# Encoder block on one core: where the second feed-forward half's weight operands are made and stored in the first half's loop, and the last norm's gain one tile later

## The chip, the cores and the metric

The kernel runs on one core of a Trainium2 chip. TensorE (PE) multiplies, VectorE (DVE), ScalarE (ACT) and GpSimd (POOL) work element by element, and SyncE (SP) issues most of the transfers between DRAM and SBUF. Each engine takes its instructions in order; between engines there are semaphores. The metric is the device time of one execution in microseconds (us).

## The reference

One transformer layer in float32 on a sequence of 1024 tokens and a width of 1024. Cut to the part that the change touches, the channel sub-layer:

```
h = modulate(layer_norm(x), sh2, sc2)                  # 1024 x 1024
gt, up = jnp.split(h @ w_ffn_in[l], 2, axis=-1)        # 1024 x 2816 each
y = (jax.nn.silu(gt) * up) @ w_ffn_out[l]              # w_ffn_out 2816 x 1024
x = layer_norm(ALPHA * x + g2[:, None, :] * y, ln2_g[l], ln2_b[l])
```

Ahead of it stands the mixer sub-layer (differential attention and multi-scale pooling), which the change leaves alone.

## The kernel before

A float32 product is made of three products of rounded halves: an operand is cast to its high part on ScalarE, VectorE subtracts that from the operand to get the low part (`split`, L96 and L97), and `mm3` multiplies high by high, high by low and low by high (L100 to L102). On top of this both feed-forward products run in Strassen's scheme, with seven products of sums of blocks instead of eight of blocks.

The first half (h times `w_ffn_in`, SiLU, gating) is a loop over 22 pairs f of 128 gate and 128 up columns. Its order on all five engines is written out by hand (`tc.manual_schedule`). Pair f multiplies its own five operands (`prod`, 12 products of 128x128x512 each) and makes the operands of pair n = f + 1 meanwhile: sums of weight blocks (`ws`) on GpSimd and VectorE, then `operand`, a `split` into `oh` and `ol`. From pair 4 (`BR`) on a pair begins with two more chains of 12 products (`first_mm`), so that it has 84 products in place of 60.

At the start of such a pair ScalarE copies the first chain's bank (`first_cp`, L929), VectorE adds the second (`first_add`, L934), and `half_gate` takes a tanh of the sum (L1238). PE can start the chain into the other half of the second bank once that add is done. Then PE's chains and their readers alternate: the copy `u` (L1270) reads bank a, the copy `p5` (L1278) bank c, and PE overwrites a bank when its reader is done. Five operands share four buffers, so the fifth (`operand(f, blocks(f)[3])`) waits until PE has used the first.

The second half multiplies by `w_ffn_out`, and its weight operands are made in this same loop, a piece at a time, by the generator `fw_prep`: for each of 11 rounds k it loads four blocks, makes three differences on GpSimd, and gives seven operands. For each one `op` splits a block into a buffer and returns the store to `wfD` in DRAM. Buffers rotate through four tags:

```python
tag = ("whi", "fwo", "wlo", "fwo")[cnt[0] % 4]
pool, bufs = (fwp, 1) if tag == "fwo" else (wp, 2)
...
split(w[:, 0, :], w[:, 1, :], src)
return lambda: nc.sync.dma_start(wfD[q - 1, k], w.bitcast(F32))
```

`fwo` has one buffer, so every second operand needs the store of the one two steps earlier to have landed. `fw_step` first issues the store that is due (`behind_`), then makes the next operand. Pairs 1 to 3 call it three times, pairs 4 on four times, which makes 77 operands by the end of pair 20. From pair 4 on the first and third operand of a pair are `fwo`. They are called s1 to s4 below.

The second half (L1480 and around it) ends with tiles 4 to 7 of the output, one after the other as PE finishes them: `last_stats` (the residual, L1384 and L1385, and its statistics), `last_norm` (mean, and on GpSimd the root, L437 and L93, and the shift, L1391 and L1392), then `last_half` twice. For tiles 4 to 6 the upper half is normalised on ScalarE (L1396), and GpSimd multiplies by the gain and adds the bias (L1399, L1400); the other halves are done by VectorE (`affine`, L443 and L444). Each half is then sent to the output.

Of the kernel before, what the change touches and what calls it, by code (L numbers as in the profile page):

```python
# [18 lines left out]
P = 128  # L19
# [16 lines left out]
def encoder_block_kernel(  # L36
# [6 lines left out]
    nc = tc.nc  # L43
    x2 = x[0]
    out2 = out[0]
# [159 lines left out]
    with tc.tile_pool(name="pre", bufs=1, reuse_waits="tile") as pre:  # L205
# [15 lines left out]
        for i in range(4):  # L221
            t = pre.tile([P, 2, D], F32, tag="x", bufs=6, name="x%d" % i)
# [218 lines left out]
    def affine(z, st, g, b):  # L441
        m, r = st
        nc.vector.scalar_tensor_tensor(z, z, m[:, 0:1], g, op0=ALU.subtract, op1=ALU.mult)  # L443
        nc.vector.scalar_tensor_tensor(z, z, r, b, op0=ALU.mult, op1=ALU.add)  # L444
# [463 lines left out]
    def prod(ps, w, x, start, stop):  # L908
        for k in range(4):
            mm3(ps, w[0][:, k, :], w[1][:, k, :], x[0][:, k, :], x[1][:, k, :],  # L910
                start and k == 0, stop and k == 3, True)
# [245 lines left out]
    def fw_prep():  # L1157


        wt = {}  # L1160

        def load(k, i, j):
            if k < NK:
                w = fwp.tile([P, HF], F32, tag="fw%d%d" % (i, j), bufs=2 - max(i, j), name="fw%d%d_%d" % (i, j, k))
                nc.sync.dma_start(w, wfo[(i * NK + k) * P:(i * NK + k + 1) * P, j * HF:(j + 1) * HF])
                wt[k, i, j] = w

        cnt = [0]

        def op(q, k, src):  # L1170
            tag = ("whi", "fwo", "wlo", "fwo")[cnt[0] % 4]
            cnt[0] += 1
            pool, bufs = (fwp, 1) if tag == "fwo" else (wp, 2)
            w = pool.tile([P, 2, HF], F32R, tag=tag, bufs=bufs, name="fw%d_%d" % (q, k))
            split(w[:, 0, :], w[:, 1, :], src)
            return lambda: nc.sync.dma_start(wfD[q - 1, k], w.bitcast(F32))

        for ij in ((0, 0), (0, 1), (1, 1), (1, 0)):
            load(0, *ij)
        for k in range(NK):  # L1180
            w11, w12, w21, w22 = [wt.pop((k, *ij)) for ij in ((0, 0), (0, 1), (1, 0), (1, 1))]
            load(k + 1, 0, 0)
            pol(w12, w12, w11, op=ALU.subtract)
            yield op(1, k, w11)
            yield op(3, k, w22)
            pol(w22, w22, w12, op=ALU.subtract)
            yield op(5, k, w12)
            load(k + 1, 0, 1)
            pol(w11, w22, w11, op=ALU.subtract)
            yield op(2, k, w21)  # L1190
            pol(w21, w21, w22, op=ALU.subtract)
            yield op(6, k, w22)
            load(k + 1, 1, 1)
            yield op(7, k, w11)
            yield op(4, k, w21)
            load(k + 1, 1, 0)
# [2 lines left out]

    def fw_step():  # L1200

        if prep is None:
            return
        for store in behind_:
            store()
        behind_[:] = [x for x in [next(prep, None)] if x]


    raws, sums_, wg = {}, {}, {}
# [5 lines left out]
    def load_up(f):  # L1215
        if f < NF:
            raws[f] = raws[f][0], uload(f)

    def blocks(f):
        rawg, rawu = raws[f]  # L1220
        return rawg[:, 0:4, :], rawg[:, 4:8, :], rawu[:, 0:4, :], rawu[:, 4:8, :]

    def operand(f, src):
        o = (fp.tile([P, 4, P], F32R, tag="oh", bufs=4, name="oh%d_%d" % (f, len(ops_.setdefault(f, [])))),
             fp.tile([P, 4, P], F32R, tag="ol", bufs=4, name="ol%d_%d" % (f, len(ops_[f]))))
        split(*o, src)
        ops_[f].append(o)
# [8 lines left out]
    def half_gate(f, half, g):  # L1236
        th = th_tile("th%d_%d" % (f, half))
        nc.scalar.activation(th, g, AF.Tanh, scale=0.5)  # L1238
        halves[f, half] = th, g

    def half_mul(f, half):
        th, g = halves[f, half]
        nc.vector.scalar_tensor_tensor(th, th, 1.0, g, op0=ALU.add, op1=ALU.mult)

    with tc.manual_schedule(engines={nc.vector.engine, nc.gpsimd.engine, nc.tensor.engine, nc.scalar.engine,
                                     nc.sync.engine}):
        load_pair(1)
        load_up(1)
        for f in range(NF):
            n = f + 1  # L1250
            more = n < NF
            if f >= BR:
                first_mm(f, wg.pop(f))
            if more:
                sa, sb = [evp.tile([P, 4, P], F32, tag="st", bufs=2, name="ws%d_%d" % (n, i)) for i in range(2)]
                pol(sa, blocks(n)[2], blocks(n)[3], op=ALU.add)
            if f >= BR:
                first_cp(f)
                fw_step()
                first_add(f, True)  # L1260
            half_gate(f, 0, chain[f][1])
            half_mul(f, 0)
            if f > 0:
                fw_step()
                operand(f, blocks(f)[3])
                a, c11, bc = chain[f]
                c = (ps_s("fc%d" % f) if bc is None else bc)[:, HF:]
                prod(a, ops_[f][0], t2, False, False)
                u2 = ev_tile("u2_%d" % f)
                nc.scalar.copy(u2, a)  # L1270
            load_pair(f + 2)
            if more:
                vec(sb, sa, blocks(n)[0], op=ALU.subtract)
                operand(n, sb)
            if f > 0:
                prod(c, ops_[f][1], t1, True, False)
                p5 = ev_tile("p5_%d" % f)
                nc.scalar.copy(p5, c)  # L1278
            else:
                a, _, c, u2, p5 = chain[f]  # L1280
            if more:
                vec(sb, blocks(n)[1], sb, op=ALU.subtract)
            fw_step()
            prod(a, ops_[f][2], t3, False, False)
            if BR <= n < NF:
                wg[n] = [wp.tile([P, KT, P], F32R, tag=tag, bufs=2, name="wg%d_%s" % (n, tag)) for tag in ("whi", "wlo")]
                nc.scalar.copy(wg[n][0], raws[n][0])
            vec(p5, p5, a, op=ALU.add)
            if more:
                operand(n, sa)  # L1290
                pol(sa, blocks(n)[0], blocks(n)[2], op=ALU.subtract)  # L1291
            if n in wg:
                vec(wg[n][1], raws[n][0], wg[n][0].bitcast(F32), op=ALU.subtract)
            load_up(f + 2)
            prod(c, ops_[f][3], b22, False, True)
            vec(u2, u2, c, op=ALU.add)
            if more:
                operand(n, sa)
            half_gate(f, 1, u2)
            prod(a, ops_[f][4], t4, False, True)  # L1300
            half_mul(f, 1)
            half_out(f, 1, p5)
            if more:
                operand(n, sb)
            if f == NF - 1:
                while behind_:
                    fw_step()
                out_ops = first_out()
            half_out(f, 0, a)
            fw_step()  # L1310
            if f == 0:
                hrs.close()
                fwp = hp.enter_context(tc.tile_pool(name="fwp", bufs=1, side="right", reuse_waits="tile"))
                prep = fw_prep()
    hp.close()


# [4 lines left out]
    with tc.tile_pool(name="fo", bufs=1, reuse_waits="tile") as fo:  # L1322
# [72 lines left out]
        def norm_act(z, st):  # L1395
            nc.scalar.activation(z, z, AF.Identity, bias=st[2], scale=st[1])  # L1396

        def gain_pool(z, cs):
            pol(z, z, l2g[:, cs], op=ALU.mult)  # L1399
            pol(z, z, l2b[:, cs], op=ALU.add)  # L1400
# [27 lines left out]
            if t < 3:  # L1428
                st_[4 + t] = shift(st_[4 + t])

        def last_half(t, cs, ap):
            z = zhi[:, t, cs]
            if ap:
                norm_act(z, st_[4 + t])
                gain_pool(z, cs)
            else:
                affine(z, st_[4 + t][0:2], l2g[:, cs], l2b[:, cs])
            (nc.scalar if cs is hi_ else nc.sync).dma_start(out2[(4 + t) * P:(5 + t) * P, cs], z)

        st_ = {}  # L1440

# [25 lines left out]
        def evac(q, t):  # L1467
            lo, hi = zlo[:, t, lo_], zlo[:, t, hi_]
            if q == 2:
                nc.scalar.copy(lo, b[t])  # L1470
            elif q == 1:
                vec(lo, lo, a[t], op=ALU.add)
            elif q == 5:
                nc.scalar.copy(e3[:, t, :], b[t])
            elif q == 6:
                nc.scalar.copy(hi, a[t])
            elif q == 3:
                vec(hi, hi, b[t], op=ALU.add)
            elif q == 7:
                vec(zhi[:, t, hi_], e3[:, t, :], a[t], op=ALU.add)  # L1480
            else:
                last_stats(t)
                last_norm(t)
                last_half(t, hi_, t < 3)
                last_half(t, lo_, False)

        late = {7: 2, 4: 7}
        first_, final = (2, 1, 5), (2, 3, 4)
# [69 lines left out]
```

## Time and profile before

| | |
|---|---|
| median of 3 timed runs | 1653.89 us (1651.23 to 1655.17) |
| profiled execution, its own time | 1650.27 us |
| its span | 1648.5 us |
| PE busy | 1566.8 us, 95% of the span |
| DVE busy | 1147.6 us, 70% |
| ACT busy | 702.1 us, 43% |
| POOL busy | 351.4 us, 21% |
| mean granted clock of PE | 0.986 |

The busy times are sums over stages with different limits. PE's products overlap: one is shown as 0.39 us long while the next starts 0.227 us later. The span is the time from the first to the last instruction; the execution's own time lies 1.8 us around it.

### The profile page before, as it was taken

What the parts mean: (1) busy time and instruction counts of PE and PEld (TensorE: products, weight loads), DVE (VectorE), ACT (ScalarE), POOL (GpSimd) and SP (SyncE); (2) the same over time, 40 slices, a digit from 0 to 9 for tenths busy, and PEclk for the clock granted to TensorE, in tenths of its full rate; (3) what the DMA queues carried; (4) which work ended last, traced back from release to release, by engine and by line L of the source; (5) the groups of instructions that cost most, each with busy time, mean ns of one, the idle gap of its engine ahead of it and who ended that gap; (6) DMA issues with size and microseconds to landing.
All of it is one profiled execution on the core that took longest, in us unless ns stands there. A gap on an engine that the chain in (4) does not pass through costs nothing. (4 is left out here: it accounts for less than half of the span.)

```text
span 1648.5 us, 20700 instructions
## 1 busy us (share of the span) xinstructions
PE 1566.8 (95%) x7634; PEld 1300.7 (79%) x7634; DVE 1147.6 (70%) x1690; ACT 702.1 (43%) x1224; POOL 351.4 (21%) x361
## 2 busy tenths in 40 slices
PE   5899999999999999999989987999999999999996
PEld 3787888888888888888878765777778778888885
DVE  7675868596876767576676797766767777436487
ACT  4445545454545445454451443444444444322220
POOL 4300001010101212000052264433333333100013
PEclk9999999999999999999999998999999999999998
DMA  9244424152423333122254523666566665897673
GB/s 332 66 119 142 118 89 130 58 136 82 116 83 109 129 98 111 58 65 66 64 165 162 177 77 102 228 206 217 202 217 226 205 229 185 315 398 249 199 266 129
DMA packets 186998, 260.77 MB, mean 158 GB/s; under 512 B 9681, under 2 KB 127506, under 8 KB 186898
## 3 DMA queue, kind: packets, MB, share of 16 engines
q1 hardware_dynamic: 181488, 244.75, 45.3%
q0 software_dynamic: 2448, 9.44, 1.5%
q10 hardware_dynamic: 2962, 5.27, 0.9%
q8 instruction: 60, 0.98, 0.2%
q14 instruction: 40, 0.33, 0.1%
HBM read 173.97 MB, written 77.07 MB: 152 GB/s over the span
## 5 line engine op out<-in xcount | busy, mean ns | idle before, releaser
L638 ACT ACTIVATE e<-e,nm 128x1024 f32<-128x1024 f32 x128 | 147.1, 1151 | 113.3 <-DVE nm L636 112.0
L636 DVE CUSTOM_DVE_ANT_0 e<-s,table 128x1024 f32<-128x1024 f32 x128 | 153.1, 1217 | 23.5 <-PE s L631 23.1
L97 DVE TENSOR_TENSOR fw<-fw,fw 128x512 fp32r<-128x512 f32 x77 | 64.7, 841 | 62.4 <-ACT fw L96 62.4
L629 PE MATMUL s<-k,q 128*128 128x512 f32 x256 | 105.2, 411 | 1.2 <-DVE nm L636 1.2
L97 DVE TENSOR_TENSOR al<-at,ah 128x512 fp32r<-128x512 f32 x128 | 83.2, 684 | 29.5 <-ACT ah L96 28.9
L96 ACT CAST oh<-ws 128x512 fp32r<-128x512 f32 x88 | 54.2, 618 | 112.0 <-POOL ws L1291 65.8
L631 PE MATMUL s<-k,q 128*128 128x512 f32 x256 | 101.6, 397 | 0.0
L97 DVE TENSOR_TENSOR ol<-ws,oh 128x512 fp32r<-128x512 f32 x88 | 65.3, 742 | 41.5 <-ACT oh L96 41.5
L643 DVE SCALAR_TENSOR_TENSOR e<-e,c,e 128x1024 f32<-128x1024 f32 x64 | 87.0, 1360 | 1.9
L96 ACT CAST ah<-at 128x512 fp32r<-128x512 f32 x128 | 70.0, 596 | 24.7 <-PE at L652 24.7
L100 PE MATMUL fa<-oA,oh 128*128 128x512 f32 x176 | 70.0, 398 | 7.9 <-ACT u L1270 5.0
L1291 POOL TENSOR_TENSOR ws<-rg,ru 128x512 f32<-128x512 f32 x21 | 43.3, 2064 | 153.0 <-DVE ol L97 102.3
L96 ACT CAST fw<-fw 128x512 fp32r<-128x512 f32 x77 | 47.4, 615 | 64.7 <-DMA wfD<-fw 54.7
L100 PE MATMUL av<-ah,vh 128*128 128x256 f32 x256 | 73.9, 289 | 0.3 <-ACT ah L96 0.2
L652 PE MATMUL at<-ident,e 128*128 128x128 f32 x512 | 68.9, 275 | 5.3 <-DVE e L643 3.2
L102 PE MATMUL av<-ah,vl 128*128 128x256 f32 x256 | 72.6, 284 | 0.0
L101 PE MATMUL av<-al,vh 128*128 128x256 f32 x256 | 72.5, 283 | 0.0
L101 PE MATMUL fa<-oA,oh 128*128 128x512 f32 x176 | 69.7, 396 | 0.5 <-DVE oA L1052 0.5
L102 PE MATMUL oa<-w,mol 128*128 128x512 f32 x176 | 68.6, 390 | 1.2 <-DVE mol L97 1.2
L102 PE MATMUL fa<-oA,ol 128*128 128x512 f32 x176 | 69.5, 395 | 0.1
L100 PE MATMUL oa<-w,moh 128*128 128x512 f32 x176 | 68.6, 390 | 0.0
L101 PE MATMUL oa<-w,moh 128*128 128x512 f32 x176 | 68.5, 389 | 0.0
(573 smaller groups left out, 4635.8 us busy)
## 6 DMA issues: line engine op xcount, KB each, us to landing
wfD<-fw SPq DMA_DIRECT2D x77, 512.0 KB, 3.7
w<-wfD SPq DMA_DIRECT2D x77, 512.0 KB, 5.4
ada<-in_w_ada_dram SPq DMA_DIRECT2D x32, 512.0 KB, 3.8
rg<-in_w_ffn_in_dram SPq DMA_DIRECT2D x26, 512.0 KB, 4.4
ru<-in_w_ffn_in_dram SPq DMA_DIRECT2D x22, 512.0 KB, 3.8
fw<-in_w_ffn_out_dram SPq DMA_DIRECT2D x44, 256.0 KB, 4.6
midD<-th SPq DMA_DIRECT2D x42, 256.0 KB, 2.0
q<-q SPq DMA_DIRECT2D x32, 256.0 KB, 3.0
```

Of the source, the lines that this page charges most:

```text
L96: nc.scalar.copy(hi, src)
L97: (eng or nc.vector).tensor_tensor(lo, src, hi.bitcast(F32), op=ALU.subtract)
L100: nc.tensor.matmul(ps, lh, rh, start=start, stop=False, skip_group_check=skip)
L101: nc.tensor.matmul(ps, lh, rl, start=False, stop=False, skip_group_check=skip)
L102: nc.tensor.matmul(ps, ll, rh, start=False, stop=stop, skip_group_check=skip)
L629: nc.tensor.matmul(ps[:, cs], q[:, 0, jj * P:(jj + 1) * P], kd[h, m][:, cs], start=True, stop=False)
L631: nc.tensor.matmul(ps[:, cs], q[:, 1, jj * P:(jj + 1) * P], kd[h, m][:, cs], start=False, stop=True)
L636: nc.vector.tensor_tensor_reduce(out=t, in0=ps, in1=table[:, o0:o0 + S], scale=-slope, scalar=3.0e38, op0=ALU.add, op1=ALU.min, accum_out=nm)
L638: nc.scalar.activation(t, t, AF.Exp, bias=nm, scale=-1.0, accum_out=zt[:, m, j:j + 1])
L643: nc.vector.scalar_tensor_tensor(s[1], s[1], c1, s[0], op0=ALU.mult, op1=ALU.add)
L652: nc.tensor.matmul(pt[:, i, :], a[:, kt * P:(kt + 1) * P], ident, start=True, stop=True, is_transpose=True)
L1291: pol(sa, blocks(n)[0], blocks(n)[2], op=ALU.subtract)
```

## The change

In the loop: `fw_step` now only makes an operand, and a new function `fw_store` issues the stores that are due. The generator gets a stop behind its first four loads, so that these are issued in pair 0 as before. The first call of a pair moves from between `first_cp` and `first_add` to behind `half_mul`; the pair's fifth operand moves ahead of `half_mul`; the second call moves behind operand 0 of the next pair, the third behind the wide split `wg` and the load of the next up block, the fourth ahead of the last `half_out`. Stores are issued at four places of their own.

In the last norm the gain of tile t (`last_gain`) is issued behind the statistics and the root of tile t + 1, and tile 7 does its lower half first.

```diff
         for ij in ((0, 0), (0, 1), (1, 1), (1, 0)):
             load(0, *ij)
+        yield None
         for k in range(NK):
...
     def fw_step():
 
-        if prep is None:
-            return
-        for store in behind_:
-            store()
-        behind_[:] = [x for x in [next(prep, None)] if x]
+        if prep is not None:
+            behind_.extend(x for x in [next(prep, None)] if x)
+
+    def fw_store():
+        while behind_:
+            behind_.pop(0)()
...
             if f >= BR:
                 first_cp(f)
-                fw_step()
                 first_add(f, True)
             half_gate(f, 0, chain[f][1])
+            if f > 0:
+                operand(f, blocks(f)[3])
             half_mul(f, 0)
+            if f >= BR:
+                fw_step()
             if f > 0:
-                fw_step()
-                operand(f, blocks(f)[3])
                 a, c11, bc = chain[f]
...
             if more:
                 vec(sb, sa, blocks(n)[0], op=ALU.subtract)
                 operand(n, sb)
+            fw_store()
+            if f > 0:
+                fw_step()
             if f > 0:
                 prod(c, ops_[f][1], t1, True, False)
...
                 vec(sb, blocks(n)[1], sb, op=ALU.subtract)
-            fw_step()
             prod(a, ops_[f][2], t3, False, False)
...
             if n in wg:
                 vec(wg[n][1], raws[n][0], wg[n][0].bitcast(F32), op=ALU.subtract)
+            fw_store()
             load_up(f + 2)
+            fw_step()
             prod(c, ops_[f][3], b22, False, True)
...
             half_out(f, 1, p5)
             if more:
                 operand(n, sb)
+            fw_store()
+            fw_step()
             if f == NF - 1:
-                while behind_:
-                    fw_step()
+                fw_store()
                 out_ops = first_out()
             half_out(f, 0, a)
-            fw_step()
+            fw_store()
             if f == 0:
...
                 prep = fw_prep()
+                next(prep)
...
+        def last_gain(t):
+            gain_pool(zhi[:, t, hi_], hi_)
+            last_out(t, hi_)
...
                 last_stats(t)
                 last_norm(t)
-                last_half(t, hi_, t < 3)
-                last_half(t, lo_, False)
+                if t < 3:
+                    norm_act(zhi[:, t, hi_], st_[4 + t])
+                if t > 0:
+                    last_gain(t - 1)
+                last_half(t, lo_)
+                if t == 3:
+                    last_half(t, hi_)
```

On ScalarE at the start of pair 8, before (`fw_3` are casts of round 3's operands, s1, s2 and s3 here; `oh_4` is the pair's fifth operand, `oh_0` the next pair's first; the copies of `p_8` are first that of `first_cp`, then p5):

```order
L929 COPY p_8_9847<-fa_9818 128x512
L96 CAST fw_3_9851<-fw_3_9581 128x512
L1238 ACTIVATE th_0_9855<-p_8_9847 128x512
L96 CAST fw_3_9861<-fw_3_9374 128x512
L96 CAST oh_4_9864<-ru_9608 128x512
L1270 COPY u_8_9880<-fa_9818 128x512
L96 CAST oh_0_9885<-ws_1_9845 128x512
L1278 COPY p_8_9901<-fb_9819 128x512
L96 CAST fw_3_9905<-fw_3_9686 128x512
```

and of the changed kernel at the same place (s1 and s2):

```order
L929 COPY p_8_9848<-fa_9819 128x512
L1240 ACTIVATE th_0_9851<-p_8_9848 128x512
L96 CAST oh_4_9853<-ru_9603 128x512
L96 CAST fw_3_9859<-fw_3_9605 128x512
L1273 COPY u_8_9874<-fa_9819 128x512
L96 CAST oh_0_9879<-ws_1_9846 128x512
L96 CAST fw_3_9886<-fw_3_9399 128x512
L1284 COPY p_8_9901<-fb_9820 128x512
```

The first cast moved from ahead of the tanh to ahead of the copy u, the second from there to ahead of the copy p5, and the third out of this piece. VectorE's subtractions move with the casts.

On SyncE's queue around the end of pair 8, before (`th_1_9949` and `th_0_9855` are the pair's half results; the store of `fw_3_9905` is that of s3, `fw_4_9978` of s4, `fw_4_10013` and `fw_4_10022` of pair 9's s1 and s2):

```order
L106 DMA ru_9930<-in_w_ffn_in_dram 128x8x128
L1232 DMA midD<-th_1_9949 128x512
L1232 DMA midD<-th_0_9855 128x512
L1176 DMA wfD<-fw_3_9905 128x1024
L1165 DMA fw_4_9973<-in_w_ffn_out_dram 128x512
L1165 DMA fw_5_9975<-in_w_ffn_out_dram 128x512
L1176 DMA wfD<-fw_4_9978 128x1024
L1176 DMA wfD<-fw_4_10013 128x1024
L106 DMA rg_10043<-in_w_ffn_in_dram 128x8x128
L1176 DMA wfD<-fw_4_10022 128x1024
```

and of the changed kernel (s3 is `fw_3_9929`, s4 `fw_4_9976`, pair 9's s1 and s2 `fw_4_10021` and `fw_4_10047`):

```order
L106 DMA ru_9927<-in_w_ffn_in_dram 128x8x128
L1234 DMA midD<-th_1_9949 128x512
L1176 DMA wfD<-fw_3_9929 128x1024
L1165 DMA fw_4_9971<-in_w_ffn_out_dram 128x512
L1165 DMA fw_5_9973<-in_w_ffn_out_dram 128x512
L1234 DMA midD<-th_0_9851 128x512
L1176 DMA wfD<-fw_4_9976 128x1024
L106 DMA rg_10038<-in_w_ffn_in_dram 128x8x128
L1176 DMA wfD<-fw_4_10021 128x1024
L1176 DMA wfD<-fw_4_10047 128x1024
```

The third operand's store moved from behind both half results to between them, and the next pair's first store from ahead of the gate load `rg` to behind it.

On GpSimd in the last norm, before, from the gain of tile 4 on (`n_5rs` is tile 5's root):

```order
L1399 TENSOR_TENSOR m_12045<-m_12045,mA 128x512
L1400 TENSOR_TENSOR m_12045<-m_12045,mB 128x512
L437 TENSOR_SCALAR n_5rs<-n_5mv 128x1
L93 TENSOR_TENSOR n_5rs<-n_5rs,mhalf 128x1
L1391 TENSOR_TENSOR nmr<-n_5mv,n_5rs 128x1
L1392 TENSOR_SCALAR nmr<-nmr 128x1
```

and of the changed kernel:

```order
L437 TENSOR_SCALAR n_5rs<-n_5mv 128x1
L93 TENSOR_TENSOR n_5rs<-n_5rs,mhalf 128x1
L1400 TENSOR_TENSOR nmr<-n_5mv,n_5rs 128x1
L1401 TENSOR_SCALAR nmr<-nmr 128x1
L1408 TENSOR_TENSOR m_12045<-m_12045,mA 128x512
L1409 TENSOR_TENSOR m_12045<-m_12045,mB 128x512
```

The two gain steps of tile 4 moved from ahead of tile 5's root to behind its shift.

## Rows read from the trace of the kernel before

**Rows 1.** Windows: pairs 1-3, 4-21, 7, 8; length, busy us (instructions), PEclk, DMA.
```profile
1016.58:1064.92 48.34, 42.32 (x181) 33.40 (x180) 36.07 (x45) 19.64 (x36) 17.75 (x11) 1.00 0.63 212
1064.92:1422.60 357.68, 348.03 (x1514) 283.72 (x1512) 241.07 (x336) 154.20 (x267) 116.45 (x73) 1.00 0.63 216
1125.66:1144.70 19.04, 19.04 (x85) 15.77 (x84) 12.79 (x19) 8.35 (x15) 7.64 (x5) 1.00 0.62 216
1144.70:1168.04 23.34, 20.97 (x85) 16.82 (x84) 14.79 (x20) 9.13 (x16) 6.45 (x5) 0.93 0.54 184
```

**Rows 2.** Waits of PE, 1005 to 1432 us: total us, times, longest us.
```profile
PE fb L100 <- DVE p L934: 9.5, 8, 2.4
...
PE fa L100 <- ACT u L1270: 5.0, 2, 2.6
```

**Rows 3.** Timeline of pair 8, rows of SP, ACT, DVE and PE: start us, us.
```profile
1148.65 0.43 SPq L1176 DMA_DIRECT2D wfD<-fw  x1
...
1153.40 0.62 ACT L96 CAST fw<-fw 128x512 fp32r<-128x512 f32 x1 [5.19 <-DMA wfD<-fw]
...
1154.05 0.69 DVE L97 TENSOR_TENSOR fw<-fw,fw 128x512 fp32r<-128x512 f32 x1 [4.40 <-ACT fw L96]
1154.66 0.68 DVE L934 TENSOR_TENSOR p<-p,fb 128x512 f32<-128x512 f32 x1
...
1155.40 0.50 PE L100 MATMUL fb<-o,oh 128*128 128x512 f32 x1 [2.37 <-DVE p L934]
```

**Rows 4.** Waits of ACT, 1005 to 1432 us.
```profile
ACT oh L96 <- POOL ws L1291: 65.8, 21, 3.6
...
ACT fw L96 <- DMA wfD<-fw: 54.7, 17, 5.2
```

**Rows 5.** DMA issues of pairs 4 to 21: count, KB, median us to landing.
```profile
wfD<-fw SPq DMA_DIRECT2D x70, 512.0 KB, 3.4
```

**Rows 6.** Timeline of pair 1, rows of ACT, PE and DVE.
```profile
1023.13 0.62 ACT L96 CAST fw<-fw 128x512 fp32r<-128x512 f32 x1 [5.36 <-DMA fw<-in_w_ffn_out_dram]
...
1024.17 0.58 ACT L1270 COPY u<-fa 128x512 f32<-128x512 f32 x1
...
1024.80 0.50 PE L100 MATMUL fa<-oA,oh 128*128 128x512 f32 x1 [2.61 <-ACT u L1270]
...
1026.07 0.68 DVE L1273 TENSOR_TENSOR ws<-ws,rg 128x512 f32<-128x512 f32 x1
...
1026.86 0.62 ACT L96 CAST oh<-ws 128x512 fp32r<-128x512 f32 x1 [2.12 <-DVE ws L1273]
```

**Rows 7.** Timeline of pair 21, rows of DVE and ACT.
```profile
1409.27 0.69 DVE L934 TENSOR_TENSOR p<-p,fb 128x512 f32<-128x512 f32 x1 [2.80 <-PE fb L102]
...
1411.73 0.62 ACT L96 CAST oh<-ru 128x512 fp32r<-128x512 f32 x1 [1.11 <-PE fa L101]
1412.26 0.58 ACT L1270 COPY u<-fa 128x512 f32<-128x512 f32 x1
...
1412.39 0.69 DVE L97 TENSOR_TENSOR ol<-ru,oh 128x512 fp32r<-128x512 f32 x1 [1.04 <-ACT oh L96]
```

**Rows 8.** Timeline of pair 7, one row of POOL and one of DVE.
```profile
1135.48 1.62 POOL L1186 TENSOR_TENSOR fw<-fw,fw 128x512 f32<-128x512 f32 x1 [4.50 <-issue]
...
1135.86 1.78 DVE L1273 TENSOR_TENSOR ws<-ws,rg 128x512 f32<-128x512 f32 x1
```

**Rows 9.** Timeline of the last norm, rows of DVE, POOL and PE.
```profile
1625.12 0.78 DVE L444 SCALAR_TENSOR_TENSOR m<-m,n_4rs,mB 128x512 f32<-128x512 f32 x1 [0.77 <-POOL n_4rs L93]
...
1628.58 1.68 POOL L1400 TENSOR_TENSOR m<-m,mB 128x512 f32<-128x512 f32 x1
...
1635.03 0.39 PE L102 MATMUL oa<-w,mol 128*128 128x512 f32 x1
...
1637.93 0.68 DVE L1384 TENSOR_TENSOR m<-oa,mA 128x512 f32<-128x512 f32 x1
...
1643.20 0.75 DVE L444 SCALAR_TENSOR_TENSOR m<-m,n_7rs,mB 128x512 f32<-128x512 f32 x1 [2.10 <-POOL n_7rs L93]
```

More of the change, by code (lines that the diff above doesn't have):

```diff
@@ L1429, in last_norm, with last_out, last_half @@
                 st_[4 + t] = shift(st_[4 + t])
[L1431 to L1438, printed above, removed]
+        def last_out(t, cs):
+            (nc.scalar if cs is hi_ else nc.sync).dma_start(out2[(4 + t) * P:(5 + t) * P, cs], zhi[:, t, cs])
+        def last_half(t, cs):
+            affine(zhi[:, t, cs], st_[4 + t][0:2], l2g[:, cs], l2b[:, cs])
+            last_out(t, cs)
+        def last_gain(t):
+            gain_pool(zhi[:, t, hi_], hi_)
+            last_out(t, hi_)
         st_ = {}
```

## The prediction

> **What bounds the kernel now.** I read the windows by stage first, cut at starts of TensorE's (PE's) products [rows 1]; the reader is to see how much longer a stretch is than its products. Pair 7 ran its 84 products without a wait in 19.04 us, 0.2267 us each. Pairs 4 to 21, 18 of them, need 342.72 us at that rate and last 357.68: 14.96 us are lost. Pairs 1 to 3 have 180 products, 40.80 us, and last 48.34: 7.54 us lost. The granted clock is 1.00 in both long stretches to two places, so the loss is waits and what follows them. Whatever the change does in the loop, it can win these 22.5 us and no more.
>
> PE's list of waits names what ended them [rows 2]: the add L934, 8 times and 9.5 us, and the copy L1270, 2 times and 5.0 us. The remaining 8 us are what each wait drags along. Pair 8 shows that [rows 1, 3]: it is 4.30 us longer than pair 7 with 2.37 us of idle time; its granted clock of 0.93 over 23.34 us is worth 1.63 us (a spell at the 1.2 GHz level behind that wait), and 0.3 us go with the restart.
>
> Why is L934 late? Pair 8, which starts at 1144.70, in order of time [rows 3]: the store of a placed operand is issued at 1148.65, behind both stores of the half results. ScalarE's cast into the same buffer starts at 1153.40, 4.75 us later, when that store has landed; VectorE's subtraction for it follows at 1154.05; only then comes L934, at 1154.66, and PE starts at 1155.40. So PE waits for a store to DRAM, through two in-order queues. ScalarE waited for such stores 17 times, 54.7 us in all [rows 4], once in nearly each of these pairs. Pair 1 has the same shape with a load instead: the cast waits until 1023.13 for its weight block, the copy L1270 stands behind it at 1024.17, and PE starts at 1024.80 [rows 6].
>
> **The change, part by part.** The loop keeps its 77 casts, subtractions and stores, so there is no work term, only waits.
>
> First operand of a pair (s1), from ahead of L934 to behind the half multiply. The add then waits for its own inputs alone. Pair 21 places nothing and shows when these come. It starts 19.04 us ahead of 1422.60, the end of the stretch in rows 1, at 1403.56; L934 comes 5.71 us in, the cast of the fifth operand 8.17, the copy u 8.70, the fifth operand's subtraction 8.83 [rows 7]. PE may start 0.74 us behind the add's start (1154.66 to 1155.40), at 6.45, and wants to after 36 products, at 8.16: 1.7 us spare. That ends the 8 waits, all of the 14.96 us if nothing takes their place.
>
> What stands behind s1 now is the copy u. Cast and copy follow each other after 0.53 us (1411.73 to 1412.26), so s1's cast is at 8.70, u at 9.23, and PE, 0.63 us behind it (1024.17 to 1024.80), at 9.86. It wants that after 48 products, at 10.88: 1.0 us spare. This holds if the store that s1 waits for has landed by 9.7. In pair 8 it was issued 3.95 us in; now it stands behind one half result, not two, at about 2.9. The median landing of these stores is 3.4 us [rows 5] and pair 8's was 4.75, so it lands at 6.3 to 7.7. I price s1 at nothing. Its cover is those 2 us; a later landing costs PE its excess over 9.7.
>
> Second operand (s2), from ahead of the fifth operand to behind operand 0 of the next pair. Behind it stands the copy p5 (L1278, L1284 in the new file). VectorE: the fifth operand's subtraction at 8.83, then half multiply, s1, the sum ws, 0.61 us each (1154.05 to 1154.66): ws at 10.66. The cast that reads ws starts 0.79 us later (1026.07 to 1026.86 [rows 6]), at 11.45; s2's cast 11.98, the copy 12.51, PE 13.14. It wants it after 60 products, at 13.60: 0.46 us spare. This is the thinnest place of the new order.
>
> Third and fourth operands, to behind the pair's wide cast and behind its last operand. The third reuses s1's buffer: s1's subtraction ends at 10.7, and its store lands 3.4 to 4.75 us later, at 14.1 to 15.5. Next on ScalarE is the cast that waits for GpSimd's difference in every pair, 21 times, 65.8 us [rows 4], 3.1 us each. The third operand's wait lies inside this one; if that cover were gone, the third would hold ScalarE 1 to 2 us, still 5 us ahead of the next pair's first copy.
>
> Pairs 1 to 3 lose the cast ahead of u. In pair 1 the block still lands at 1023.1, now with p5 behind the cast, at 1023.65; PE without its wait of 2.6 us would want that at about 1024.7. So the 7.54 us go as well.
>
> Loop: 14.96 + 7.54 = 22.5 us, of which I leave 1.5 us to short new waits at the thin place: 21.0.
>
> The tail. GpSimd's two gain steps of a tile, 1.68 us the second, stood ahead of the next tile's root. VectorE waited 2.10 us for tile 7's root, where tile 4, with no gain ahead, waited 0.77. It started tile 7 at 1637.93, though PE's last product ended at 1635.42, 2.5 us earlier [rows 9]. With the gains one tile later tile 7 can at best start on time (2.5 us) and wait 0.77 (1.3 us): 3.8 us less. But the gains then run beside VectorE's own steps. In pair 7 a VectorE sum of two SBUF tiles started at 1135.86, inside a GpSimd operation that ended at 1137.10, and took 1.78 us, ending 0.54 us after it [rows 8]; its like takes 0.69 [rows 3]. Three such steps stand on the tail's chain (the residuals of tiles 6 and 7, tile 7's affine step), each up to 1.1 us longer: 0.5 us left. I take 1.5 us, nearer to the locked row, since a gain step lasts longer than a VectorE step.
> The Trainium skill, "GPSIMD Engine Reference" (1. Specifications), has the two engines share their SBUF interface, with contention where a VectorE instruction has two SBUF inputs; the row agrees. By that rule the tail comes out near the low end, or as in D.
>
> Sum: 21.0 + 1.5 = 22.5 us. The profiled execution took 1650.27 us (1.8 us around its span), which gives 1627.8. The timed runs' median is 1653.89, 3.6 us above it; on their scale it is 1631.4. I predict 1631; if all waits go and the tail is free, 22.5 + 3.8 = 26.3, it is 1627.6 there and 1624 on the profile's scale.
>
> **Rivals.**
> A, the thin place gives way. GpSimd catches ws or a step ahead of it, as in pair 7: 1.1 us more, so 0.6 us of waiting for p5 and 0.3 of restart. For: GpSimd's own weight differences wait for a subtraction of just these operands and start right behind it. Against: ws starts 0.61 us after s1, before s1 has ended. Six such pairs cost 5.4 us, all 21 cost 19: 1637 to 1650, in the middle 1643.
>
> B, the wait only changes its place, from L934 to u. For no change each of the 21 pairs must lose the 1.07 us that it lost before, so the store must land at 9.7 + 0.8 = 10.5 us in (0.3 is restart), 7.6 us after issue. Against: 4.75 us in the worst pair looked at. 1650 to 1657.
>
> C, slower: the same place from that point on. s1's cast holds u, the next pair's first operand, s2 and p5 in one queue; with landings of 9 us each pair loses 2.5 us, 52 in all, less the 22.5: 1683. For: half result, store, loads, half result, store now follow each other closely on one queue. Against: before, five transfers did too.
>
> D, the tail gives nothing: tile 5's gain, locked by VectorE's steps, ends 1 to 2 us late, tile 7's root with it, and tile 6's gain, at least 3.3 us behind that root, ends after tile 7's own output. It is worked out from rows 8 and 9: a root as late as 1641.5, 1.7 us before the old one, and two steps of 2.2 us end at 1645.9, 0.5 us after the old last step (three of 0.75 us from 1643.20 on). 1633.4.
>
> **How the numbers follow.** Forecast 0.50 (1624 to 1637), D 0.25 with the same loop, A 0.17, B 0.04, C 0.04. The range 1625 to 1642 holds the forecast, D and the better half of A, some 8 in 10, with the best case on the runs' scale at its foot. 0.2% is 3.3 us, about what a measurement of this kernel can tell from no change; forecast, D and nearly all of A are beyond it: faster 0.91, same 0.05, slower 0.04.
>
> **What would show it.** Right: PE's list of waits without L934 and u; pairs 4 to 21 in 343 to 346 us; ScalarE waiting for stores at the third operand and hardly at s1; VectorE's waits for the roots of tiles 5 to 7 under 1.5 us. Wrong: a PE wait on p5 (A); s1's cast later than 9.7 us into a pair (B, C); the end set by GpSimd's last gain (D).

## The result and the profile after

The changed kernel takes 1628.13 us (median of 4 runs, 1626.53 to 1630.31), the kernel before in the same comparison 1652.56 us (4 runs, 1650.03 to 1655.17). The ratio is 0.9853, with a 95% interval of 0.9832 to 0.9874: faster by 1.5%. The profiled execution took 1627.82 us around a span of 1626.0, where that of before had 1650.27 and 1648.5.

The windows of the kernel after, cut at the same products as [rows 1], with the same columns: pairs 1 to 3, pairs 4 to 21, pair 7, pair 8.

```profile
1016.62:1058.44 41.82, 41.56 (x181) 34.03 (x180) 34.07 (x46) 20.18 (x36) 18.18 (x11) 0.99 0.69 235
1058.44:1401.16 342.72, 342.72 (x1513) 283.79 (x1512) 263.46 (x336) 156.24 (x266) 123.22 (x74) 1.00 0.65 227
1115.56:1134.60 19.04, 19.04 (x85) 15.77 (x84) 13.77 (x20) 9.05 (x16) 6.26 (x4) 1.00 0.69 236
1134.60:1153.64 19.04, 19.04 (x85) 15.77 (x84) 15.95 (x20) 8.95 (x16) 8.12 (x6) 1.00 0.65 223
```

In the second row length and PE's busy time are the same number: PE has not one gap in pairs 4 to 21. Pair 8, 23.34 us before, now lasts what pair 7 lasts. PE's list of waits, 1005 to 1412 us, is complete with three rows:

```profile
PE fa L100 <- DVE p L1293: 5.2, 1, 5.2
PE ob L102 <- DVE m_ol L97: 0.3, 1, 0.3
PE fc L100 <- ACT p L1284: 0.3, 1, 0.3
```

L934 and the copy u (now L1273) are gone from it [rows 2]; the 5.2 us belong to pair 0, where the kernel before waits 5.1, and the copy p5 (L1284) stands there once, in pair 2. ScalarE's waits of the same stretch:

```profile
ACT oh L96 <- POOL ws L1296: 44.9, 21, 3.6
...
ACT fw L96 <- DMA wfD<-fw: 5.7, 9, 1.4
```

The wait for stores fell from 54.7 us to 5.7 [rows 4]. All nine that are left are those of the third operand, which stands ahead of the cast that waits for GpSimd, and the wait for GpSimd fell beside them, from 65.8 to 44.9. The stores themselves are no quicker, their median landing is still 3.4 us [rows 5]:

```profile
wfD<-fw SPq DMA_DIRECT2D x70, 512.0 KB, 3.4
```

The timeline of the tail: PE's last product, VectorE's steps from tile 7's residual on, and GpSimd's last gain steps:

```profile
1613.58 0.39 PE L102 MATMUL oa<-w,mol 128*128 128x512 f32 x1
...
1614.30 0.68 DVE L1393 TENSOR_TENSOR m<-oa,mA 128x512 f32<-128x512 f32 x1
1615.01 1.23 DVE L1394 SCALAR_TENSOR_TENSOR m<-mA,m 128x512 f32<-128x512 f32 x1
...
1618.76 1.74 DVE L444 SCALAR_TENSOR_TENSOR m<-m,n_7rs,mB 128x512 f32<-128x512 f32 x1 [0.76 <-POOL n_7rs L93]
1620.42 1.75 DVE L443 SCALAR_TENSOR_TENSOR m<-m,n_7mv,mA 128x512 f32<-128x512 f32 x1
1622.20 0.75 DVE L444 SCALAR_TENSOR_TENSOR m<-m,n_7rs,mB 128x512 f32<-128x512 f32 x1
...
1618.69 1.26 POOL L1408 TENSOR_TENSOR m<-m,mA 128x512 f32<-128x512 f32 x1
1620.03 1.59 POOL L1409 TENSOR_TENSOR m<-m,mB 128x512 f32<-128x512 f32 x1
```

The wait for tile 7's root is 0.76 us in place of 2.10 [rows 9], but three VectorE steps that start inside a GpSimd step take 1.23 to 1.75 us; such a step is called locked below.

How the 22.4 us between the two spans (1648.45 and 1626.04) divide, with the same stretches of every experiment. The marks are PE's first product of pair 1, of pair 4 and of the second half, and its last product; the tail runs from there to the end of the span. What lies ahead of pair 1 took between 1014 and 1019 us from trace to trace, in kernels that differ only behind it, so stretches are safer to compare than totals.

| kernel | pairs 1-3 | pairs 4-21 | second half | tail |
|---|---|---|---|---|
| before | 48.34 | 357.68 | 212.43 | 13.43 |
| changed | 41.82 | 342.72 | 212.42 | 12.46 |
| loop_only | 41.60 | 342.72 | 212.45 | 13.43 |
| tail_only | 48.34 | 359.45 | 212.42 | 12.20 |
| s1_ahead_of_add | 42.78 | 351.00 | 212.42 | 12.46 |
| store_earlier | 47.69 | 342.72 | 212.43 | 13.49 |
| place_alone | 42.48 | 345.26 | 212.40 | 12.48 |
| store_late | 41.41 | 472.95 | 212.46 | 12.93 |
| two_more_copies | 41.41 | 355.81 | 212.43 | 12.20 |
| tail_mean_first | 41.39 | 342.72 | 212.46 | 11.91 |
| no_last_gain | 42.40 | 342.72 | 212.44 | 10.21 |

Changed against before: 6.52 in pairs 1 to 3, 14.96 in pairs 4 to 21, 0.97 in the tail. Only the second of the three is sharp. Five of the kernels have the same loop in pairs 1 to 3 (changed, loop_only, two_more_copies, tail_mean_first, no_last_gain) and took 41.39 to 42.40 there; six have the same last norm (changed, tail_only, s1_ahead_of_add, place_alone, store_late, two_more_copies) and took 12.20 to 12.93.

### The profile page after: what moved, and what is told of

The parts are those of the page before. It is cut to its first block, busy times and chain, and to the rows that moved or that the text cites. A ratio compares the mean times of both kernels' runs of the same rounds, so it can differ in the third digit from the quotient of the medians.

```text
span 1626.0 us, 20759 instructions
## 1 busy us (share of the span) xinstructions
PE 1564.6 (96%) x7634; PEld 1305.5 (80%) x7634; DVE 1170.9 (72%) x1690; ACT 705.2 (43%) x1224; POOL 359.1 (22%) x361
## 5 line engine op out<-in xcount | busy, mean ns | idle before, releaser
L96 ACT CAST oh<-ws 128x512 fp32r<-128x512 f32 x88 | 54.0, 616 | 85.7 <-POOL ws L1296 44.9
L97 DVE TENSOR_TENSOR ol<-ws,oh 128x512 fp32r<-128x512 f32 x88 | 73.5, 835 | 21.1 <-ACT oh L96 21.1
L97 DVE TENSOR_TENSOR fw<-fw,fw 128x512 fp32r<-128x512 f32 x77 | 82.1, 1066 | 0.2 <-ACT fw L96 0.2
L652 PEld LDWEIGHTS at<-ident,e 128*128 128x128 f32 x512 | 59.4, 145 | 11.0 <-DVE e L643 3.6
```

The source lines that it names most:

```text
L96: nc.scalar.copy(hi, src)
L97: (eng or nc.vector).tensor_tensor(lo, src, hi.bitcast(F32), op=ALU.subtract)
L652: nc.tensor.matmul(pt[:, i, :], a[:, kt * P:(kt + 1) * P], ident, start=True, stop=True, is_transpose=True)
```

## The experiments

**Half of the change each.** loop_only has the new loop and the last norm of before; tail_only has the old loop and the new last norm.

> The changed loop with the old last norm. By the prediction's sum: pairs 4 to 21 in 342.7 us and pairs 1 to 3 in about 42 us as in the changed kernel, the last norm as before; the profiled span is 1 us longer than the changed kernel's 1626.0, so 1627. If the last norm brought more than its 1 us, or the two parts depend on each other, the span is 1630 or more.

> The old loop with the changed last norm. By the prediction: pairs 4 to 21 stay near 357.7 us; from PE's last product's start to the end of the span 12.4 us in place of 13.5; span 1647 to 1648. If the tail is what wins, the span falls by 5 us or more.

loop_only: 1629.20 us (1627.53 to 1630.87), ratio 0.9869 [0.9854, 0.9884]. Its loop is the changed kernel's and its tail, 13.43, that of before. Its profiled span is 1629.1 and not 1627, since what lies ahead of pair 1 took 2.2 us longer in this trace. tail_only, one execution: 1648.47 us; its tail is 1.23 us shorter, its loop still waits for L934 nine times. The two halves don't touch each other, and the loop is some 95% of the gain.

**Which place matters: s1 back ahead of the add.** The rest of the change stays.

```diff
                 first_cp(f)
+                fw_step()
                 first_add(f, True)
...
             half_mul(f, 0)
-            if f >= BR:
-                fw_step()
```

> The changed kernel with one place undone: a pair's first operand stands ahead of the add L934 again, the stores stay where the change puts them. The add is late when the cast starts later than 8.16 - 0.74 - 0.61 - 0.65 = 6.2 us into the pair. If the place alone makes the gain, pairs 4 to 21 lose 13 to 15 us again. If the earlier store alone makes it, nothing is lost. If both count, as I now think: stores issued 2.4 to 2.8 us in land by 6 and cost nothing, and the four pairs whose store is issued at 3.8 to 4.7 lose 1 to 2 us each, 4 to 8 us in all.

1636.83 us (1635.01 to 1637.34), ratio 0.9913 [0.9897, 0.993]; pairs 4 to 21 give back 8.28 of the 14.96 us, a little over what I expected. PE's waits of this kernel:

```profile
PE fb L100 <- DVE p L934: 4.4, 5, 2.3
```

The pairs sort themselves by one number, the start of s1's cast. Read from the timeline of each pair, in us from its start: at 5.72 and earlier (nine pairs) a pair takes 19.04; at 6.06 it takes 19.16, at 6.37 19.39, at 6.54 19.57, at 7.82 20.83, at 8.58 23.19. So the old place loses time from a cast at about 6.0 on, and from there each microsecond costs about one, more in the last of these pairs, where the mean granted clock is 0.93. With the new place the cast never has to be that early.

**The store earlier, nothing else.** To the kernel before, with all its old places, one loop is added that issues the due store ahead of the load of the next up block.

```diff
+            while behind_:
+                behind_.pop(0)()
             load_up(f + 2)
```

> The kernel before with one change: the third operand's store is issued ahead of the load of the next up block, not behind the half results; every operand is made where it was before. If the wait is for the landing of that store, as predicted, the cast finds it landed: pairs 4 to 21 in 343 to 346 us, pair 1 keeps its 2.6 us wait for a weight block, 16 to 18 us faster in all. If the place of the operands is what matters, PE still waits for L934 and the gain is under 4 us.

1634.17 us (1633.93 to 1635.93), ratio 0.9902 [0.9887, 0.9916]. All 18 pairs take 19.04 us, s1's cast starts at 3.40 in each of the 17 that have one, still ahead of the add, and ScalarE waits for no store there. The window of pairs 4 to 21 and the cast in pair 8, which starts at 1141.67:

```profile
1065.51:1408.23 342.72, 342.72 (x1514) 283.88 (x1512) 255.95 (x336) 156.63 (x267) 116.66 (x73) 1.00 0.65 225
```
```profile
1145.07 0.62 ACT L96 CAST fw<-fw 128x512 fp32r<-128x512 f32 x1
```

These two lines of code alone win the whole 14.96 us of pairs 4 to 21. What they don't win is pairs 1 to 3 (47.69), where a load, not a store, holds the cast ahead of u; I had expected the wait of 2.6 us there to stay, and other losses of that stretch stayed with it.

**The places, without the earlier store.** In the changed kernel the `fw_store` ahead of the last `fw_step` is taken out, so that s3's store is issued behind both half results again.

> The changed kernel with only the places moved: the third operand's store stays behind both half results, as before. It is then issued 4 to 7 us into the pair and lands, 3.1 to 4.8 us later, at 7 to 10, against the 9.7 that the new place of s1 allows. By the prediction's margin pairs 4 to 21 take 343 to 347 us, with a loss in the one or two pairs whose half result is latest. If the store had to move too, they take 350 us or more.

1632.11 us (1631.82 to 1632.32), ratio 0.9878 [0.9861, 0.9894]; pairs 4 to 21 take 345.26, so the places alone win 12.42 of the 14.96. s1's cast now waits for its store in seven pairs, in pair 8 longest. ScalarE's and PE's rows there (pair 8 starts at 1136.06, so that the cast is 11.07 us in):

```profile
1147.13 0.62 ACT L96 CAST fw<-fw 128x512 fp32r<-128x512 f32 x1 [2.27 <-DMA wfD<-fw]
1147.65 0.58 ACT L1273 COPY u<-fa 128x512 f32<-128x512 f32 x1
```
```profile
1148.29 0.50 PE L100 MATMUL fa<-oA,oh 128*128 128x512 f32 x1 [1.18 <-ACT u L1273]
```

This is rival B's wait, on u. It begins where I had put it: with casts at 9.05 to 9.52 us a pair takes 19.04 to 19.06, at 9.84 19.32, at 10.33 19.79, at 11.07 20.52. The limit that I worked out was 9.7. Three pairs lose more than 0.1 us, where I had expected one or two.

**Rival C provoked: the stores late.** In the changed kernel, from pair 4 on, the stores of s3 and s4 are issued behind the next pair's gate load, some 10 us into it, and that load stands ahead of s1's place.

```diff
             half_mul(f, 0)
             if f >= BR:
+                load_pair(f + 2)
+                fw_store()
                 fw_step()
...
-            load_pair(f + 2)
+            if f < BR:
+                load_pair(f + 2)
...
-            fw_store()
             fw_step()
...
-            fw_store()
+            if f + 1 < BR or f + 2 >= NF:
+                fw_store()
```

> The changed kernel with the third and fourth operands' stores issued behind the next pair's load rg, at 10.0 us into it (pairs 4 on). Rival C on purpose: s1's cast then starts at 13.4 or later, u 0.5 behind it, PE at 14.6 or later against 10.88: 4 to 5 us in each of 17 pairs with the restart, 68 to 85 us slower than the changed kernel, pairs 4 to 21 in 411 to 428 us, and PE waits on the copy u. If a late store costs nothing there, the margin in the prediction is not what protects u.

1759.44 us (1758.91 to 1759.71), ratio 1.0648 [1.0632, 1.0664]: slower, as C said, but by more than I expected: pairs 4 to 21 last 130.2 us longer than in the changed kernel. Its waits of PE, and the windows of pairs 4 to 21 and of pair 12:

```profile
PE fa L100 <- ACT u L1275: 87.4, 16, 5.7
```
```profile
1059.59:1532.54 472.95, 385.55 (x1514) 310.44 (x1512) 263.11 (x336) 157.75 (x266) 123.64 (x74) 0.88 0.47 164
1276.25:1303.51 27.26, 21.75 (x85) 17.47 (x84) 15.17 (x20) 8.92 (x16) 6.34 (x5) 0.87 0.47 162
```

The waits for u are 87.4 us, 5.5 in each of 16 pairs. In pair 12 the stores are issued at 1286.25, s3's first, and s1's cast starts 5.4 us later:

```profile
1286.25 1.05 SPq L1176 DMA_DIRECT2D wfD<-fw  x2
```
```profile
1291.66 0.62 ACT L96 CAST fw<-fw 128x512 fp32r<-128x512 f32 x1 [6.59 <-DMA wfD<-fw]
```

The other 42.8 us are 2.7 per pair, in which PE is busy: pair 12 has 21.75 us of busy time for 84 products that take 19.04 in the changed kernel, at a mean granted clock of 0.87. Its first product behind the wait takes 0.80 us, where that behind a wait in place_alone took 0.50, and the granted clock from 1293 to 1297 us is 0.50, the lower of the two levels (1.2 GHz):

```profile
1292.81 0.80 PE L100 MATMUL fa<-oA,oh 128*128 128x512 f32 x1 [5.51 <-ACT u L1275]
```

I had expected 4 to 5 us a pair, and 8.1 came. About 2 of the difference are the landing, 5.4 us behind the issue where I had put 3.4; the rest is what follows the wait, which I had priced at a restart of 0.3.

**The thin place.** Two more copies of 128x512 on ScalarE, whose result nobody reads, ahead of p5 in pairs 4 to 20.

```diff
+                for i in range(2 if BR <= f < NF - 1 else 0):
+                    nc.scalar.copy(fwp.tile([P, HF], F32, tag="dmy", bufs=1, name="dmy%d_%d" % (f, i)), u2)
                 p5 = ev_tile("p5_%d" % f)
```

> The changed kernel with two more ScalarE copies of 128x512 ahead of the copy p5 in pairs 4 to 20; their results are not read. By the prediction's working p5 starts 12.5 us into the pair and has 0.5 us spare; two copies of 0.52 us move it to 13.5, PE gets it at 14.2 in place of 13.60: 0.55 us idle and 0.3 restart in each of 17 pairs, 14 us slower than the changed kernel. If p5 has more room than worked out (over 1 us), nothing is lost.

1642.63 us (1639.8 to 1643.04), ratio 0.994 [0.9923, 0.9957]; pairs 4 to 21 take 13.09 us more. Now PE waits for p5 in each of the 17 pairs:

```profile
PE fb L100 <- ACT p L1286: 8.0, 17, 0.5
```

13.09 / 17 is 0.77 us of loss per pair. The copy p5 and PE's product behind it in pair 7, which starts at 1120.17:

```profile
1133.77 0.58 ACT L1286 COPY p<-fb 128x512 f32<-128x512 f32 x1
```
```profile
1134.40 0.50 PE L100 MATMUL fb<-oB,oh 128*128 128x512 f32 x1 [0.46 <-ACT p L1286]
```

p5 is 13.60 us into the pair in place of 12.47, 1.13 later, and PE's product at 14.23 in place of 13.60, 0.63 later: 0.50 us of spare time, where I had worked out 0.46. (The wait of 0.46 is counted from the shown end of the product before, which lies 0.16 behind the point at which the next could start.) Rival A's place is real; in pairs 4 to 21 of the changed kernel nothing pushed it over.

**The tail.** tail_mean_first lets tile 7 subtract its mean in both halves before it needs the root. no_last_gain leaves out GpSimd's gain and bias for tile 6's upper half, so that this part of the output is only normalised.

> The changed kernel; for the last tile both first affine steps (they need the mean alone) stand ahead of both second ones (they need the root). The second of the two runs in the 0.76 us in which VectorE waits for the root. If the end is VectorE's chain, span 0.7 to 0.8 us shorter than 1626.0. If GpSimd's gain sets the end, no change.

> The changed kernel without GpSimd's gain and bias for tile 6's upper half (that part of the output is only normalised). VectorE's affine steps for tile 7 took 1.74 and 1.75 us beside that gain, 0.78 and 0.75 elsewhere. If they wait for GpSimd's interface to SBUF, both fall to about 0.77 and the span is 1.9 us shorter; if they are slow for another reason, they stay at 1.7.

no_last_gain, one execution: 1627.83 us, its tail 10.21, 2.25 us shorter than the changed kernel's. Its whole span is no shorter, 1626.0, since pairs 1 to 3 and what lies ahead of them took 2.2 us longer in this trace. The same two steps of VectorE, with no GpSimd step beside them:

```profile
1620.77 0.75 DVE L444 SCALAR_TENSOR_TENSOR m<-m,n_7rs,mB 128x512 f32<-128x512 f32 x1 [0.76 <-POOL n_7rs L93]
1621.43 0.75 DVE L443 SCALAR_TENSOR_TENSOR m<-m,n_7mv,mA 128x512 f32<-128x512 f32 x1
```

0.75 us each in place of 1.74 and 1.75: the gain steps beside them were the cause. That is 2.0 us; the other 0.25 come from tile 7 starting that much sooner behind PE's last product.

tail_mean_first: 1626.95 us (1624.91 to 1628.43), ratio to the kernel before 0.985 [0.9835, 0.9865]. Its tail is 0.55 us shorter than the changed kernel's where I expected 0.7 to 0.8, and 0.26 of this is again an earlier start of tile 7, so that the new order of the steps won 0.29. GpSimd's root took longer there, 0.93 us in place of 0.57, and both root steps are still locked (3.41 us for the two):

```profile
1617.29 1.42 DVE L1505 SCALAR_TENSOR_TENSOR m<-m,n_7mv,mA 128x512 f32<-128x512 f32 x2
1619.17 3.41 DVE L1507 SCALAR_TENSOR_TENSOR m<-m,n_7rs,mB 128x512 f32<-128x512 f32 x2 [0.46 <-POOL n_7rs L93]
```
```profile
1618.20 0.93 POOL L93 TENSOR_TENSOR n_7rs<-n_7rs,mhalf 128x1 f32<-128x1 f32 x1
```

It has the lowest median of all the versions, but its interval overlaps that of the changed kernel; the 0.55 us are read from one trace of each.

## Why the prediction was right, point by point

**What bounds the loop.** Right. PE waited through ScalarE's and VectorE's queues for a store's landing. s1_ahead_of_add brings L934 back with that wait, store_earlier and place_alone remove the same loss from two sides: the landing earlier, or the waiting cast out of the way.

**The worked order of a pair.** Right. In pairs of the changed kernel L934 starts 5.71 us in (6.26 at the latest), s1's cast at 8.71, u at 9.23, the sum ws at 10.65, s2's cast at 11.95, p5 at 12.47. I had 5.71, 8.70, 9.23, 10.66, 11.98 and 12.51, taken from pair 21 of before, which places nothing, and single durations. Pair 8 in the timelines of VectorE and ScalarE (it starts at 1134.60):

```profile
1145.24 0.69 DVE L1276 TENSOR_TENSOR ws<-ws,rg 128x512 f32<-128x512 f32 x1
```
```profile
1143.40 0.62 ACT L96 CAST fw<-fw 128x512 fp32r<-128x512 f32 x1
1143.93 0.58 ACT L1273 COPY u<-fa 128x512 f32<-128x512 f32 x1
...
1146.55 0.62 ACT L96 CAST fw<-fw 128x512 fp32r<-128x512 f32 x1
1147.07 0.58 ACT L1284 COPY p<-fb 128x512 f32<-128x512 f32 x1
...
1150.49 0.62 ACT L96 CAST fw<-fw 128x512 fp32r<-128x512 f32 x1 [1.38 <-DMA wfD<-fw]
1152.15 0.62 ACT L96 CAST oh<-ws 128x512 fp32r<-128x512 f32 x1 [1.04 <-POOL ws L1296]
```

s1 (the first row of the cast) does not wait; the third operand waits 1.38 us for its buffer and then GpSimd's difference is still 1.04 us away, as the step on its cover had it. s3's store was issued 2.4 to 2.8 us into most pairs, which I had at 2.9, up to 4.7 in a few.

**Pairs 4 to 21.** 14.96 us, all of it, and none of the 1.5 us that I kept for short new waits was needed there.

**Pairs 1 to 3.** I expected all of 7.54; 6.52 came. That is the term that was over-sized. Two things make up the 1.02 us that stay: the wait of 0.26 for p5 in pair 2, 0.58 with its restart, and, for the other 0.44, a spell at the lower clock level behind pair 0's wait of 5.2 us, which ended just ahead of pair 1 before and reaches into it now: the first three products take 1.12 us (1016.62 to 1017.74) in place of 0.68. I had taken over the granted clock of 1.00 that this stretch had before. The spell is this trace's: in the other four with the same loop it ends ahead of pair 1. The wait for p5 is in all five, 0.26 to 1.07 us long, and it is the mechanism of rival A: in pair 2 VectorE's half multiply starts inside a GpSimd difference, takes 1.77 us in place of 0.68, and the sum ws behind it, the casts and p5 come that much later.

```profile
1034.06 1.11 DVE L97 TENSOR_TENSOR ol<-ru,oh 128x512 fp32r<-128x512 f32 x1
1035.09 1.77 DVE L1245 SCALAR_TENSOR_TENSOR th<-th,p 128x512 f32<-128x512 f32 x1
1036.78 0.68 DVE L1276 TENSOR_TENSOR ws<-ws,rg 128x512 f32<-128x512 f32 x1
...
1034.58 1.73 POOL L1190 TENSOR_TENSOR fw<-fw,fw 128x512 f32<-128x512 f32 x1
```

Of the 1.5 us that I kept back from the loop for short new waits at the thin place this took 0.58, and the spell 0.44, for which I had nothing: the loop comes to 21.5, against 21.0 predicted.

**The tail.** 0.97 us against 1.5. The start of tile 7 came 2.18 us sooner behind PE's last product (0.72 us behind its start in place of 2.90), and the root's wait fell by 1.34: 3.52 us. Three locked steps took back 2.5: tile 7's residual, 1.23 us in place of 0.69 for the same step before, and two of its affine steps, 1.74 and 1.75 in place of 0.75 [rows 9]. I had three such steps, at up to 1.1 us each, but took tile 6's residual for one of them and only one affine step; tile 6's is locked too, and that shows only as a start of tile 7 0.33 us behind the end of PE's last product. The Trainium skill, "GPSIMD Engine Reference" (1. Specifications), has GpSimd share its SBUF interfaces with VectorE, with contention where a VectorE instruction has two SBUF inputs. The trace agrees, 1.74 us with the gain step and 0.75 without it. What came lies midway between the low end of 0.5 that I worked out with three locked steps and the 1.5 that I took, so I gave the locked steps too little weight.

**The sum.** 22.5 us predicted and 22.5 measured between the two profiled executions (1650.27 less 1627.82); that it agrees so closely is luck, since the loop gave 0.5 more and the tail 0.5 less than their terms. On the scale of the medians the prediction was 1631, the result 1628.13; 1.3 of these 3 us are that the median I started from, 1653.89, was of three runs and is above that of the comparison, 1652.56. The medians of the comparison differ by 24.4 us, the two profiled executions by 22.5; the stretch ahead of pair 1 scatters by more than this difference, and I have not followed it further.

**The rivals.** A (the thin place): once, in pair 2, 0.26 us. B and C (the wait moves to u): not at all, and place_alone and store_late show both as soon as the store is late. Their margin was the store's new place, which I treated as a condition of the move; for pairs 4 to 21 it is by itself enough. D (the tail gives nothing): it was VectorE's steps that were held and not GpSimd's. The gain steps took 1.26 and 1.59 us, where D had 2.2 each and the kernel before 1.43 and 1.68, and tile 6's gain ended at 1621.62 (1620.03 and 1.59), 1.33 us ahead of the end of VectorE's last step (1622.20 and 0.75).

**What I missed.** I costed the change as one order and did not ask which part of it was needed. The stall had two ends, a late landing and a queue behind it. For pairs 4 to 21 the earlier store alone was enough, and the new places alone won 12.42 of the 14.96 us.

## What to carry to other kernels

An instruction that needs a buffer back from DRAM should not stand, in an in-order queue, ahead of one that another engine's matmuls wait for; find such places by following a PE wait through the queue of the engine named, to the first instruction there that waits for a DMA. Then try the cheap end first: issue the store of a single-buffered tile as soon as it is made. The new order can be timed from the old trace, by a stretch without the moved work and single durations, to within 0.1 us per step, and the smallest spare time in it says what to test next.

## What the runs showed that I had not expected

A wait of 5.5 us for PE cost 8.1 us: store_late lost 87.4 us in waits and 42.8 us more in products at a mean granted clock of 0.88. It does not take many waits, or long ones. In pair 8 of s1_ahead_of_add a single wait of 2.26 us cost 4.15, at a mean granted clock of 0.93, while a wait of 2.29 us in pair 5 of the kernel before cost 2.59, at 1.00. What decides between the two I have not followed. Two of the locked VectorE steps of the tail end 0.55 us after the GpSimd step that they started in (1620.50 after 1619.95, and 1622.17 after 1621.62), as in [rows 8], where it was 0.54. And the landing of the same 512 KB stores differed between the orders: a median of 3.4 us in the changed kernel, 4.0 in place_alone and 4.2 in store_late.
